# Seven-product stage of 17 granules, scores with a minimum per component, and other units in attention and memory of a hybrid trunk layer

## The chip, the cores and the metric

The kernel runs on one core of a Trainium2 chip. The metric is the device time of one execution in microseconds (us). TensorE (PE in the profile) multiplies matrices, VectorE (DVE) and ScalarE (ACT) work on what it leaves and prepare what it reads, GpSimd (POOL) and SyncE (SP) mostly issue DMAs.

## The reference, cut to what matters

One layer of a trunk over 640 tokens (512 latent tokens and 128 context tokens) of width 1024, in float32:

```python
x = x + 0.5 * m[2] * swiglu(hh, ffn1_w1, ffn1_w3, ffn1_w2)          # d_ff = 2816
mq, mk, mv, mo, mg, dq, dk, dv, gm, gd = split_cols(h @ w_in)
dq, dk = rope_2d(rmsnorm(dq)), rope_2d(rmsnorm(dk))                  # latent tokens only
pr = softmax(q_c . k_c * scale)  for components c = 0, 1             # 8 heads, 768 or 128 keys
att = (pr[0] - lam * pr[1]) @ v
h_f, h_b = mlstm_chunkwise(q, k, v, log_i, log_f, state)             # 4 heads of 256, both directions
hm = rmsnorm(h_f + h_b) * sigmoid(mo)
y = sigmoid(gm) * (hm @ w_br_m) + sigmoid(gd) * (att @ w_br_d)
x = x + m[5] * (y @ w_out)
x = x + 0.5 * m[8] * swiglu(hh, ffn2_w1, ffn2_w3, ffn2_w2)
```

The modulation vectors m come from silu(c) @ w_ada, a matrix of 1024 x 9216. The result must hold to float32 accuracy, so a product is made of three matmuls on split operands (high times high, high times low, low times high).

## The kernel before, in words

**Helpers.** Nearly every operation goes through a helper and carries its line: L54 is a DVE operation on two tensors, L57 one with a scalar as well, L61 one of a tensor and scalars, L51 an ACT activation, L75 a matmul, L78 a transpose by PE, L97 a load by SP. So groups are told apart by their tiles. DVE, ACT, PE and SP each work through their instructions in the order in which the program has them.

**Seven-product granules.** Large products are done as a two by two block product with seven products in place of eight (class `Winograd`). A granule is 256 output columns: 7 products of 12 matmuls 128x320 each, 84 in all. For that the weights are summed and split: ACT and DVE make `ww` (128x2048), `wB` (128x1024) and `wC` (128x512) out of the landed `raw`, and DVE forms the sums in `raw` (one add of 128x1024, two of 128x512). `u` and `t` are results of products on their way through ACT and DVE. In the same shape without that scheme, a granule is 4 units of 24 matmuls 128x320 (a feature unit) or 5 units of 24 matmuls 128x256 (a token unit).

**The stages in order of time** (read from the timelines): an opening (to about 90 us); FFN1's up products (to about 312); FFN1's down products (312 to 465), of which the middle part is four seven-product granules, `mid[0]` to `mid[3]`; the second norm and the first query and key projections (to about 505); the class `Gates`, a seven-product stage of 12 granules (505 to 655); attention (655 to 1079); the mLSTM ("memory", 1079 to 1210); the branch and output projections (to 1388); FFN2 (to the end).

**Gates** (L1783) computes gate columns for three of four groups (`gd`, `gm`), the four opening gates (`o`) and one query and one key granule of the mLSTM. Results go to DRAM (`g_out`). `between` (L1901) puts other work between its products: the rope (`qk_norm_rope`, L1470) of the first head pair's queries after granule 2 and of its keys after granule 3, and from granule 5 on four column tiles at the places `IN_GATES` (L1918). What the Tile scheduler makes of it is the order shown below.

**Column tiles** (`Columns`, L788): 56 tiles of 128 columns of the modulation product that are needed later. Each is a 512 KB load and two DVE operations over 128x1024 with a sum (L814, with a short read of the accumulator behind each). They are put wherever DVE has room: 11 in FFN1's up products, 9 and 4 in its down products (`TILES`, L1166, by granule and place), 4 in Gates, 8 in the memory stage (L2187), the rest in FFN2.

**Attention** walks 8 heads; a head has 5 blocks of 128 queries (`qi`). In a block: `scores` (L1597, 8 matmuls into a tile `sc` of 1536 columns over three PSUM banks, component 0 in its first half and component 1 in its second, then one minimum over both, L1617), `soft` (two exponentials on ACT, into tiles `p`, which read the minimum), `mix` on DVE, `turn` (6 transposes, `ps_wT`), `values` (12 matmuls, `ps_o`). The minimum, the exponentials and the mix stand between the matmuls of a block, so PE needs other work meanwhile: a queue of units (`Fill`), built from L1752 on, of which `UNITS` (L1954) says how many go into each block: mostly one in even heads, two in the first blocks of odd heads. The queue holds value projections (token units), keys and queries of pairs 1 to 3 (token units, each followed by its rope), and mLSTM queries and keys of heads 1 to 3 (feature units). At the end of a head the next head's `queries` and `keys` are turned; an odd head puts five single units there, an even one a group at each of three places. All of it shares a pool `ps2` of 5 PSUM banks.

**Memory** (class at L2037): for each of 4 heads a table `P` is loaded as a broadcast, masked, exponentiated and multiplied by key-query products (`prep`, `ps_st`), then 10 cells follow each other (`cell`). Three granules of units of 12 are left for it: the last key granule and the two of the gates (12 feature units).

## Time and profile before

| what | us |
|---|---|
| runs | 1814.38, 1814.83, 1815.23 (median 1814.83) |
| the profiled execution, and its span | 1815.7, and 1813.9 |
| PE busy, weight loads busy | 98%, 96% of the span |
| DVE, ACT busy | 74%, 50% |
| chain that ended last | PE 85%, DVE 7%, DMA 4%, ACT 2%, issue 1% |

A matmul's row shows its own duration, but matmuls overlap: 12 of 128x320 in a row start and end within about 1.8 us. So what an extra matmul costs is read from a long row of them, and what PE lost is read from the idle time in a stage. An idle time of PE is followed by the engine and tile that ended it.

### The profile page before, as it was taken

To read this page: it belongs to the slowest core of one execution; us is meant where nothing else is said; L and a number is where in the kernel's file an instruction comes from. 1 tells how busy PE (TensorE), PEld (TensorE's weight loads), DVE (VectorE), ACT (ScalarE), POOL (GpSimd) and SP (SyncE) were. 2 spreads that over 40 slices of the span, in tenths; PEclk is the share of its full clock that TensorE was granted. 3 is DMA by queue.
4 is the path that set the end of the run, shared out by engine and by line. 5 is a ranking of instruction groups with operands and counts; after the bars stand their busy time and mean duration, and the time that the engine had idled before them with its cause. 6 is when DMAs were issued, how large, how long until landed. Compare 5 with 4: busy or idle time off the path is not lost.

```text
span 1813.9 us, 30780 instructions
## 1 busy us (share of the span) xinstructions
PE 1785.6 (98%) x12550; PEld 1744.6 (96%) x12550; DVE 1349.6 (74%) x2178; ACT 910.8 (50%) x1588; POOL 39.2 (2%) x69
## 2 busy tenths in 40 slices
PE   8999999999999999999999999999999999999998
PEld 6999999999999999999999998899999999999998
DVE  6879987677888765858584557977767888897485
ACT  5654544333655445556564547674336545554432
POOL 0000000100000000000000000000000000000010
PEclk9999999999999999999999999999999999999999
DMA  8355566977245434221221124576642355557992
GB/s 326 111 198 171 186 236 221 350 227 266 83 139 181 160 131 143 78 69 63 69 69 55 68 81 163 182 257 218 221 171 80 134 173 185 203 180 274 353 311 80
DMA packets 132207, 311.36 MB, mean 172 GB/s; under 512 B 10017, under 2 KB 93217, under 8 KB 119009
## 3 DMA queue, kind: packets, MB, share of 16 engines
q1 hardware_dynamic: 121122, 265.22, 42.3%
q0 software_dynamic: 10256, 41.55, 7.1%
q8 instruction: 98, 1.61, 0.4%
q10 hardware_dynamic: 688, 2.63, 0.4%
q14 instruction: 43, 0.35, 0.1%
HBM read 240.49 MB, written 68.87 MB: 171 GB/s over the span
## 4 chain that ended last, share of the span: by engine, by line
PE 85%; DVE 7%; DMA 4%; ACT 2%; issue 1%; SPq 0%; DVEq 0%; ACTq 0%
PE ps_f L75 48%; PE ps_p L75 14%; PE ps_t L75 12%; PE sc L75 2%; PE ps_n L75 2%; PE ps_o L75 2%; DVE ww L54 2%; PE ps_u L75 1%; DMA raw_a<-in_w_ada_k 1%; PE ps_wT L78 1%; PE ps_qkT L78 1%; DMA raw<-in_w2b 1%; DVE junk L814 1%; DMA P<-nm_dram 1%; DVE mn L1617 1%
## 5 line engine op out<-in xcount | busy, mean ns | idle before, releaser
L75 PE MATMUL ps_f<-S,ww 128*128 128x320 f32 x2400 | 387.5, 310 | 5.2 <-DVE ww L54 1.9
L75 PEld LDWEIGHTS ps_f<-S,ww 128*128 128x128 f32 x2400 | 359.8, 188 | 9.6 <-DVE ww L54 6.5
L54 DVE TENSOR_TENSOR ww<-raw,ww 128x2048 fp32r<-128x2048 f32 (+1 forms) x73 | 163.9, 2246 | 74.3 <-ACT ww L51 74.2
L75 PE MATMUL ps_t<-wH,hH 128*128 128x256 f32 x640 | 185.7, 290 | 0.9 <-DVE x L57 0.9
L75 PE MATMUL ps_f<-hm,ww 128*128 128x320 f32 x1176 | 185.8, 309 | 0.1
L75 PE MATMUL ps_t<-wH,hL 128*128 128x256 f32 x640 | 181.6, 284 | 0.9 <-DVE hL L54 0.9
L75 PE MATMUL ps_t<-wL,hH 128*128 128x256 f32 x640 | 181.4, 283 | 0.0
L75 PEld LDWEIGHTS ps_f<-hm,ww 128*128 128x128 f32 x1176 | 175.7, 188 | 0.6 <-DVE ww L54 0.6
L51 ACT ACTIVATE ww<-raw 128x2048 fp32r<-128x2048 f32 (+1 forms) x73 | 136.9, 1875 | 60.3 <-DVE raw L54 33.0
L54 DVE TENSOR_TENSOR raw<-raw 128x1024 f32<-128x1024 f32 x186 | 161.0, 865 | 2.2
L75 PE MATMUL ps_f<-hm,wB 128*128 128x320 f32 x1008 | 161.5, 309 | 0.0
L75 PE MATMUL ps_p<-hH,wH 128*128 128x320 f32 x480 | 151.1, 315 | 0.7 <-ACT aT L51 0.7
L75 PEld LDWEIGHTS ps_f<-hm,wB 128*128 128x128 f32 x1008 | 151.3, 188 | 0.0
L75 PE MATMUL ps_p<-hH,wL 128*128 128x320 f32 x480 | 148.3, 309 | 0.0
L75 PE MATMUL ps_p<-hL,wH 128*128 128x320 f32 x480 | 148.3, 309 | 0.0
L51 ACT ACTIVATE u<-ps_f 128x320 f32<-128x320 f32 x129 | 55.8, 433 | 161.5 <-PE ps_f L75 159.7
L75 PEld LDWEIGHTS ps_t<-wH,hH 128*128 128x128 f32 x640 | 123.0, 192 | 1.5 <-ACT nsq L51 1.1
L75 PEld LDWEIGHTS ps_t<-wH,hL 128*128 128x128 f32 x640 | 122.9, 192 | 1.1 <-DVE hL L54 1.1
L75 PEld LDWEIGHTS ps_t<-wL,hH 128*128 128x128 f32 x640 | 123.1, 192 | 0.4
L1617 DVE TENSOR_REDUCE mn<-sc 128x2 f32<-128x1536 f32 (+1 forms) x40 | 59.5, 1489 | 56.0 <-PE sc L75 55.8
L54 DVE TENSOR_TENSOR wB<-raw,wB 128x1024 fp32r<-128x1024 f32 x64 | 78.1, 1221 | 26.7 <-ACT wB L51 26.7
L51 ACT ACTIVATE wH<-raw 128x2048 fp32r<-128x2048 f32 (+1 forms) x45 | 75.4, 1681 | 42.2 <-PE ps_p L75 35.5
(309 smaller groups left out, 3621.9 us busy)
## 6 DMA issues: line engine op xcount, KB each, us to landing
g_dram<-g SPq DMA_DIRECT2D x44, 640.0 KB, 7.6
raw_a<-in_w_ada_c POOLq DMA_DIRECT2D x35, 512.0 KB, 4.7
g_dram<-g SPq DMA_DIRECT2D x24, 480.0 KB, 8.1
raw<-in_w1b SPq DMA_DIRECT2D x11, 1024.0 KB, 4.9
raw<-in_w3b SPq DMA_DIRECT2D x11, 1024.0 KB, 6.3
raw<-in_w1a SPq DMA_DIRECT2D x10, 1024.0 KB, 4.9
raw<-in_w3a SPq DMA_DIRECT2D x10, 1024.0 KB, 6.2
hm<-g_dram SPq DMA_DIRECT2D x7, 1280.0 KB, 12.5
```

Of the source, the lines that this page charges most:

```text
L51: return placed(nc.scalar.activation(*args, **kw))
L54: return placed(eng.tensor_tensor(out=out, in0=in0, in1=in1, op=op))
L75: tc.keep_in_program_order(nc.tensor.matmul(*args, **kw))
L78: tc.keep_in_program_order(nc.tensor.transpose(*args, **kw))
L814: placed(vec.tensor_tensor_reduce(out=junk, in0=raw, in1=self.csil[:, v, :], op0=ALU.mult, op1=ALU.add, scale=1.0, scalar=0.0, accum_out=m ...
L1617: placed(vec.tensor_reduce(out=mn, in_=sv, axis=AX.X, op=ALU.min))
```

## The change

It has five parts.

- **Gates**: 17 granules in place of 12. The queries of heads 1 to 3 and the keys of heads 1 and 2 of the mLSTM move there from attention's queue, store to DRAM, and are loaded again: the keys of heads 0 to 2 late in attention (`load_keys` in head 6), the queries at the start of the memory stage (`load_queries`). Seven column tiles go between the products, not four. PSUM: four banks of `ps2`, and two halves of a tile `more` that later is the score tile of component 1 (class `Six`).
- **Scores**: each component has a PSUM tile of two banks and a minimum of its own (128x768), right behind its matmuls; `ps2` has 4 banks.
- **Attention's queue**: one mLSTM key granule (head 3) is left of the feature units; every block of every head has one unit; the ends of the heads are alike. Tiles of odd pairs' keys and queries have places of their own.
- **Memory**: values of head 3 (5 token units) come ahead of the two gate granules; two column tiles in place of eight; the query loads stand ahead of others on SP's queue.
- **FFN1's down products**: 12 column tiles in place of 9; `TILES` gets one more at each of (22, 1), (23, 0) and (23, 1).

```diff
-                    columns.place(9, places[0], load_columns_down, 4)
+                    columns.place(12, places[0], load_columns_down, 4)
...
-        TILES = {(21, 0): 2, (21, 1): 2, (22, 0): 2, (22, 1): 1, (23, 0): 1, (23, 1): 1, (28, 0): 2, (28, 1): 1, (29, 0): 1}
+        TILES = {(21, 0): 2, (21, 1): 2, (22, 0): 2, (22, 1): 2, (23, 0): 2, (23, 1): 2, (28, 0): 2, (28, 1): 1, (29, 0): 1}
...
-    psum = att.enter_context(tc.tile_pool(name="ps2", bufs=5, space=PSUM))
+    psum = att.enter_context(tc.tile_pool(name="ps2", bufs=4, space=PSUM))
...
+            n, self.n = self.n % 6, self.n + 1
+            return psum.tile(shape, dtype, tag=tag, name=name) if n < 4 else self.more[:, 512 * n - 2048 : 512 * n - 1536]
...
             for c in range(2):
+                s = ps_s.tile([128, 1024], F32, tag=f"s{c}", name="sc")
                 if qi < 4:
-                    for k0, k1 in (((0, 512), (512, 768)) if c == 0 else ((0, 256), (256, 768))):
+                    for k0, k1 in ((0, 512), (512, 768)):
...
-            placed(vec.tensor_reduce(out=mn, in_=sv, axis=AX.X, op=ALU.min))
+                placed(vec.tensor_reduce(out=mn[:, c : c + 1], in_=sv[c], axis=AX.X, op=ALU.min))
...
-            rest = [(a["w_mq"], mq_dram, 0, self.query), (a["w_mk"], mk_dram, 0, self.plain)]
+            qk = [(a[n], dst, h, f) for h in range(4) for n, dst, f in (("w_mq", mq_dram, self.query), ("w_mk", mk_dram, self.plain))]
...
-            for src, dst, g, f in gate[:4] + o[:1] + rest[:1] + o[1:2] + rest[1:] + o[2:3] + gate[4:5] + o[3:] + gate[5:]:
+            for src, dst, g, f in gate[:5] + qk[:3] + o[:1] + qk[3:5] + o[1:2] + qk[5:7] + o[2:] + gate[5:]:
...
-    IN_GATES = [(i, 1) for i in (5, 7, 9, 11)]
+    IN_GATES = [(i, 1) for i in (5, 6, 7, 9, 10, 12, 13)]
...
-    UNITS = {
-        0: (two, two, two, two, one, (1, 1, 1)), 1: (two, two, two, one, one, (0,)),
...
+    UNITS = {hd: (one,) * 5 + ((1, 1, hd < 4),) for hd in range(7)}
+    UNITS[7] = (one,) * 4 + ((0, 0), (0, 0))
...
+    in_pools["q"] = queries_of.enter_context(tc.tile_pool(name="mlq", bufs=1, side="right", reuse_waits="tile"))
+    load_queries(0)
...
-    columns.place(8, csil2, load_columns_raw, 1)
+    for h in range(1, 4):
+        load_queries(h)
+    columns.place(2, csil2, load_columns_raw, 1)
...
-            if n in ((3, 7), (2, 5, 8), (2, 5, 8), ())[h]:
+            if n in ((), (5,), (5,), ())[h]:
```

The order moves at three places of which the prediction speaks. The first is DVE in FFN1's down products, behind the split `ww` of `mid[0]`, up to the split of `mid[1]`. Before:

```order
L54 TENSOR_TENSOR ww<-raw,ww 128x2048
L54 TENSOR_TENSOR wB<-raw,wB 128x1024
L54 TENSOR_TENSOR wC<-raw,wC 128x512
L54 TENSOR_TENSOR raw<-raw 128x2x4x128
L54 TENSOR_TENSOR raw<-raw 128x4x128 x2
L57 SCALAR_TENSOR_TENSOR x<-ps_f,half_m,x 128x320
L54 TENSOR_TENSOR ww<-raw,ww 128x2048
```

And in the changed kernel, from the same split on:

```order
L54 TENSOR_TENSOR ww<-raw,ww 128x2048
L814 ISA ada,mod<-ada,csil 128x1024
L814 ISA mod 128x1
L54 TENSOR_TENSOR wB<-raw,wB 128x1024
L54 TENSOR_TENSOR wC<-raw,wC 128x512
L814 ISA ada,mod<-ada,csil 128x1024
L814 ISA mod 128x1
L54 TENSOR_TENSOR raw<-raw 128x2x4x128
L814 ISA ada,mod<-ada,csil 128x1024
```

Three more such operations follow, between the two small adds of `raw` and the residual's `x` and `t`, and then `ww` of `mid[1]`. So six column operations, as many as the three added tiles have, stand between the two splits, where there was none.

The second place is DVE in Gates, around the split `ww` of granule 5, with the rope of the first pair's keys (`k_tok`, `rope`, `ss`). Before:

```order
L54 TENSOR_TENSOR k_tok<-k_tok,ry 128x1280
L54 TENSOR_TENSOR g_out<-ps_f,u 128x320
L54 TENSOR_TENSOR k_tok<-k_tok,g_kn 128x256
L54 TENSOR_TENSOR ww<-raw,ww 128x2048
L61 TENSOR_SCALAR g_out<-ps_f 128x320
L54 TENSOR_TENSOR wC<-raw,wC 128x512
L54 TENSOR_TENSOR rope<-rope,ropeBk 128x1024
L54 TENSOR_TENSOR k_tok<-k_tok,ropeAk 128x1024
```

And now:

```order
L54 TENSOR_TENSOR k_tok<-k_tok,ry 128x1280
L54 TENSOR_TENSOR k_tok<-k_tok,g_kn 128x256
L54 TENSOR_TENSOR rope<-rope,ropeBk 128x1024
L54 TENSOR_TENSOR k_tok<-k_tok,ropeAk 128x1024
L54 TENSOR_TENSOR k_tok<-k_tok,rope 128x1024
L54 TENSOR_TENSOR ww<-raw,ww 128x2048
```

The three last steps of the rope stood behind the split and now stand ahead of it. One granule earlier the same holds for the queries' rope and the split of granule 4.

The third place is SP's queue at the start of the memory stage. Before:

```order
L97 DMA mask<-in_mask 128x256
L97 DMA P<-nm_dram 128x5x128 x2
L97 DMA va<-v_dram 128x5x256
L97 DMA C<-in_c_aug 128x516 x2
L97 DMA csil<-csil_dram 128x2048
L2049 DMA P<-nm_dram 128x5x128 x2
L2052 DMA va<-v_dram 128x5x256
```

And now:

```order
L1715 DMA mqT<-mq_dram 128x1280
L97 DMA mask<-in_mask 128x256
L97 DMA P<-nm_dram 128x5x128 x2
L97 DMA va<-v_dram 128x5x256
L97 DMA C<-in_c_aug 128x516 x2
L97 DMA csil<-csil_dram 128x2048
L1715 DMA mqT<-mq_dram 128x1280 x3
L1729 DMA v_dram<-stage 128x256 x2
L2026 DMA P<-nm_dram 128x5x128 x2
L2029 DMA va<-v_dram 128x5x256
```

Four query loads of 640 KB each, and two stores of values, now stand ahead of the second head's table `P`; on DVE the masking of that table moved from ahead of the first cell to behind the fourth.

## The prediction, on record before the changed kernel had run

> **What bounds the kernel now.** I read the page first. Its line of busy times and the line of the chain that ended last say the same thing:

> ```profile
> PE 1785.6 (98%) x12550; PEld 1744.6 (96%) x12550; DVE 1349.6 (74%) x2178; ACT 910.8 (50%) x1588; POOL 39.2 (2%) x69
> PE 85%; DVE 7%; DMA 4%; ACT 2%; issue 1%; SPq 0%; DVEq 0%; ACTq 0%
> ```

> PE is the bound. A change can gain in two ways: fewer matmuls, or fewer waits of PE. How much the waits are worth shows in the windows by stage (length, then busy time of PE, PE's weight loads, DVE, ACT, POOL). The four are FFN1's down products, Gates, attention from 750, and memory.

> ```profile
> 312.00:465.00 153.00, 151.65 (x1027) 150.46 (x1025) 107.08 (x167) 57.24 (x88) 11.87 (x19) 1.00 0.80 272
> 505.00:655.00 150.00, 148.36 (x1012) 148.09 (x1011) 115.73 (x158) 73.56 (x113) 2.11 (x4) 1.00 0.49 167
> 750.00:1079.00 329.00, 323.34 (x2547) 314.37 (x2545) 212.95 (x330) 179.22 (x379) 0.00 (x0) 0.99 0.19 64
> 1079.00:1210.00 131.00, 126.99 (x727) 113.93 (x727) 107.37 (x336) 86.91 (x222) 0.00 (x0) 1.00 0.58 183
> ```

> PE is idle for 1.35, 1.64, 5.66 and 4.01 us in them, 12.7 us together. That is all that removed waits can bring in the stages that the change touches, and it also says that PE has no slack there: a DVE that comes late shows on PE at once. The list of waits of PE names them (total, times, longest):

> ```profile
> PE ps_wT L78 <- DVE p L57: 3.0, 7, 0.8
> PE ps_f L75 <- DVE ww L54: 1.9, 3, 1.6
> PE sc L75 <- ACT p L51: 1.6, 3, 0.9
> PE ps_f L75 <- DMA S<-g_dram: 0.9, 1, 0.9
> PE ps_p L75 <- ACT aT L51: 0.7, 1, 0.7
> ```

> **The matmuls that go.** Five granules of mLSTM queries and keys leave attention, where each costs 4 units of 24 matmuls, and enter Gates, where each costs 7 products of 12. That is 96 against 84, so 60 matmuls of 128x320 fewer. Nothing else in the count of matmuls changes: the value units and the key granule that change places between attention and memory are whole in both kernels. The price of one comes from long unbroken rows of the chain (start, length, what):

> ```profile
> 275.42 100.31 PE ps_f L75 x682
> 754.84 3.51 PE ps_p L75 x24
> ```

> 100.31 / 682 is 0.147 us, and 3.51 / 24 is 0.146. So 60 x 0.147 = **-8.8 us**, on the engine that is the bound. This is the firm term.

> **Three more column tiles in FFN1's down products.** They bring six operations of L814 between the splits `ww` of `mid[0]` and `mid[1]`. DVE there before (start, length, what):

> ```profile
> 365.58 1.22 DVE L814 CUSTOM_DVE_ANT_0 ada<-ada,csil 128x1024 bf16<-128x1024 f32 x1
> 369.47 2.29 DVE L54 TENSOR_TENSOR ww<-raw,ww 128x2048 fp32r<-128x2048 f32 x1 [1.40 <-ACT ww L51]
> 372.14 1.23 DVE L54 TENSOR_TENSOR wB<-raw,wB 128x1024 fp32r<-128x1024 f32 x1 [0.37 <-ACT wB L51]
> 373.28 0.69 DVE L54 TENSOR_TENSOR wC<-raw,wC 128x512 fp32r<-128x512 f32 x1
> 373.88 2.67 DVE L54 TENSOR_TENSOR raw<-raw 128x1024 f32<-128x1024 f32 x3
> 377.52 0.55 DVE L57 SCALAR_TENSOR_TENSOR x<-ps_f,half_m,x 128x320 f32<-128x320 f32 x1 [0.96 <-PE ps_f L75]
> 379.00 2.29 DVE L54 TENSOR_TENSOR ww<-raw,ww 128x2048 fp32r<-128x2048 f32 x1 [0.94 <-ACT ww L51]
> ```

> and PE where it uses what that last split leaves:

> ```profile
> 380.83 2.24 PE L75 MATMUL ps_f<-hm,ww 128*128 128x320 f32 x12
> 383.98 1.99 PE L75 MATMUL ps_f<-S,ww 128*128 128x320 f32 x12 [0.90 <-DMA S<-g_dram]
> ```

> The split ends at 381.29, and PE's product from 380.83 on already waits a little for it (2.24 us; the 12 behind it have 1.99). Neighbouring instructions of DVE overlap by some 0.08, so I count the new order from 371.7: six column operations at 1.15, `wB` 1.14, `wC` 0.6, the adds 1.14 + 0.6 + 0.6, `x` 0.5, and `t` and two pieces of `x` (about 1.0), which now stand ahead of the split. That is 12.5, so the split starts at 384.2 and ends at 386.5, 5.2 later. Its ACT half is done by then, since `raw` is complete near 381. PE has nothing else to do in between, because its order is fixed. One thing is given back: the wait of 0.90 for a transfer at 383.98 lies behind and is covered. Sum **+4.3 us**. From below it could be 3 (if `t` and `x` went quicker), from above 6 (if one of the three tiles, which GpSimd loads, lands after its turn).

> **Gates.** The 17 granules themselves are in the first term. What is new is the order of the ropes. The rows of before that matter (the rope of the keys, the split of granule 5, the late split of granule 6, and the product that needs granule 5's split):

> ```profile
> 559.21 1.49 DVE L54 TENSOR_TENSOR k_tok<-k_tok,ry 128x1280 f32<-128x1280 f32 x1
> 561.35 2.29 DVE L54 TENSOR_TENSOR ww<-raw,ww 128x2048 fp32r<-128x2048 f32 x1
> 564.55 1.22 DVE L54 TENSOR_TENSOR rope<-rope,ropeBk 128x1024 f32<-128x1024 f32 x1
> 565.69 1.22 DVE L54 TENSOR_TENSOR k_tok<-k_tok,ropeAk 128x1024 f32<-128x1024 f32 x1
> 568.36 1.22 DVE L54 TENSOR_TENSOR k_tok<-k_tok,rope 128x1024 f32<-128x1024 f32 x1
> 577.42 2.29 DVE L54 TENSOR_TENSOR ww<-raw,ww 128x2048 fp32r<-128x2048 f32 x1 [1.39 <-ACT ww L51]
> 565.35 1.92 PE L75 MATMUL ps_f<-S,ww 128*128 128x320 f32 x12
> ```

> Granule 5's split ended at 563.64, 1.7 ahead of its use at 565.35. Now three steps of 1.22 stand ahead of it, 3.4 us net. One granule earlier the queries' steps do the same to granule 4. Walking both through with these lengths, granule 4's split comes about 0.9 late and granule 5's 2.2 later still: +3.1. Against that, the wait of 1.6 for the split at 577.42, which a column tile and two gate evacuations had delayed, goes, since the first column tile now comes after granule 6's split: I take -1.7, of the stage's 1.64 idle and the 1.9 of all such waits. Sum **+1.4 us**, from -1.7 (ropes covered) to +4.

> **Attention.** The minimum is split. Its rows, and the distance of two blocks with one unit (start of the scores):

> ```profile
> L1617 DVE TENSOR_REDUCE mn<-sc 128x2 f32<-128x1536 f32 x32 | 56.2, 1756 | 54.0 <-PE sc L75 54.0
> L1617 DVE TENSOR_REDUCE mn<-sc 128x2 f32<-128x256 f32 x8 | 3.4, 420 | 2.0 <-PE sc L75 1.9
> 806.50 1.40 PE sc L75 x8
> 812.76 1.40 PE sc L75 x8
> ```

> From 0.420 at 256 columns and 1.756 at 1536, a column costs 1.04 ns and an instruction 0.153 us, so half a tile costs 0.95 and two of them 1.91. The first half can start 0.7 earlier, behind half of the scores' 1.40. So the first exponential, which waited for the whole minimum, starts about 1.5 earlier. The longest wait for `p` is 0.8 and the waits for the score tile (`sc` for `p`) are at most 0.9, so both kinds, 4.6 us, can go. The price is 32 x 0.153 = 4.9 us of DVE, which has 329 - 213 = 116 us to spare in this stretch. [...]

> New waits come too. Heads 4 to 6 have no unit between the second half of the next keys and its scores, so PE waits for an evacuation by ACT; the nearest row is `ps_p` for `aT`, 0.7, three times: +2.1. And the rope of pair 1's queries is issued one block before they are packed. Its five steps take 1.49 + 0.42 (nearest row: the minimum of 256 columns) + 3 x 1.22 = 5.6 us of DVE beside the block's own 1.9 + 1.0 + splits, in a block of 812.76 - 806.50 = 6.3: 0 to 3 late, I take 1.5. Sum -4.6 + 2.1 + 1.5 = **-1.0**, from -4.6 (nothing new) to +4.9 (old waits stay and what DVE gained in work lands on PE).

> **Memory.** Four query loads of 640 KB now lie ahead of tables. DVE's maskings before, and the DMA view for 1079 to 1102:

> ```profile
> 1087.45 0.83 DVE L54 TENSOR_TENSOR P<-P,mask 128x640 f32<-128x640 f32 x1 [1.43 <-DMA P<-nm_dram]
> 1095.74 0.82 DVE L54 TENSOR_TENSOR P<-P,mask 128x640 f32<-128x640 f32 x1 [1.90 <-DMA P<-nm_dram]
> GB/s 0 0 334 236 277 217 86 140 142 151 150 221 311 361 395 398 453 429 446 435 340 358 346 290 281 267 342 346 306 272 253 226 328 385 374 241 144 75 41 14
> DMA packets 5089, 5.99 MB, mean 260 GB/s; under 512 B 224, under 2 KB 4320, under 8 KB 4960
> ```

> A load of 0.66 MB takes 1.4 us at the best slice (453 GB/s) and 2.5 at the mean (260). So head 0's table comes 1.4 to 2.5 later, and head 1's, behind all four, 5.8 to 10.1: from about 1096.5 to between 1102 and 1107. Its masking is now behind the fourth cell. The 40 cells of the stage fill 131 us, 3.3 each, so four of them behind a first table near 1090 end near 1103; I take 1104, an estimate. Against that stand six column tiles fewer (12 x 1.15 = 14 us of DVE), which should end small waits later in the stage, and PE's units, which fill the start. Sum **+0.3**, from -2 to +4.

> **The sum.** -8.8 + 4.3 + 1.4 - 1.0 + 0.3 = -3.8 us. The profiled execution took 1815.7 (span 1813.9, and 1.8 around it) and would take 1811.9; it lies 0.9 above the median of the runs, so the forecast for the median is 1814.8 - 3.8 = **1811.0**. About 0.2% (3.6 us) is what a measurement of this kernel can tell from no change, so 1811.2 to 1818.4 counts as the same: the forecast stands on the edge.

> **Rivals.**

> *The waits go and none comes* (chance 0.22). DVE is busy for 74% only; Gates' ropes hide, attention loses its 4.6 and gets 0.5 at most. -8.8 + 4.3 - 1.7 - 4.1 = -10.3: about 1804.5. For it speaks that the exponentials start 1.5 earlier; against it, that the splits in Gates had 1.7 to spare.

> *The gain is eaten* (0.17). Attention's new waits come at their upper end (+4) while the rest holds: -8.8 + 4.3 + 1.4 + 4 = +0.9, or with FFN1 at its lower end about 0: 1814 to 1816. For it speaks the packing of heads with one unit per block throughout.

> *The second head's table comes too late* (0.15). If the queue in front of it moves at the mean of 260 GB/s or below, it lands at 1107 or later. The masking stands on DVE ahead of every later cell of head 0, so all of them wait behind it from the fourth cell's end (1104) on. It decides from 1104; each us beyond is a us of PE once the units are used up. With 2.5 for head 0's table and 4 to 6 for head 1's, -3.8 + 8 = +4.2: 1819, slower.

> **Chances.** The forecast has 0.46, with a range of its own from 1807.5 to 1814.5; half of it lies below 1811.2. Faster by over 0.2%: 0.23 + 0.22 = 0.45. The same: 0.23 + 0.17 = 0.40. Slower: 0.15. The range reaches down to the first rival and up to the third's middle: 1804 to 1819.

> **What would show it.** In FFN1's down products the split of `mid[1]` ends near 386.5 and PE shows a wait of some 4 to 5 us for `ww` near 382. Gates shows two waits for `ww` near 554 and 567, and none in its later granules. In attention `ps_wT` for `p` and `sc` for `p` fall below 1 us in all. PE's matmul count is lower by 60. The forecast is wrong if FFN1's down stage is not longer by 3 us or more (then the kernel is nearer to 1806), or if a wait for `P` or `num` of over 3 us stands near 1100.

## The result, and the profile after

The changed kernel takes 1879.74 us (median of 4 runs, 1876.98 to 1882.14) against 1815.03 for the kernel before (4 runs, 1814.38 to 1817.99): 1.0353 times as long, with a 95% interval of 1.0332 to 1.0373. It is slower by 65 us. The forecast was 1811 and its upper end 1819.

PE has its 60 matmuls fewer, but it is busy for longer, and its share of the chain fell from 85% to 78%. The page of the changed kernel:

```profile
PE 1798.5 (96%) x12490; PEld 1752.8 (93%) x12490; DVE 1381.4 (73%) x2245; ACT 926.4 (49%) x1611; POOL 42.5 (2%) x75
PE 78%; DVE 9%; ACT 5%; DMA 4%; issue 3%; SPq 0%; DVEq 0%; ACTq 0%
```

Where the time went is seen by cutting both traces at the same places of the program: the first token product, the last gate column product, the last product of Gates, the end of attention, the end of memory. The windows of the kernel before (length; busy PE, weight loads, DVE, ACT, POOL; granted clock; DMA share and rate):

```profile
0.00:466.10 466.10, 456.98 (x3135) 444.45 (x3135) 364.73 (x539) 217.88 (x323) 18.05 (x34) 1.00 0.65 225
466.10:505.20 39.10, 37.74 (x292) 36.67 (x293) 36.19 (x58) 25.43 (x48) 0.00 (x0) 1.00 0.19 67
655.20:1079.00 423.80, 418.14 (x3340) 407.83 (x3338) 276.02 (x428) 232.32 (x485) 0.00 (x0) 1.00 0.23 76
```

and of the changed kernel:

```profile
0.00:473.20 473.20, 460.35 (x3134) 447.21 (x3135) 371.07 (x551) 217.58 (x322) 19.67 (x37) 0.99 0.65 225
473.20:518.40 45.20, 39.69 (x292) 38.65 (x293) 37.67 (x59) 28.04 (x50) 0.00 (x0) 0.92 0.27 90
518.40:763.10 244.70, 220.05 (x1432) 215.84 (x1431) 158.99 (x207) 99.56 (x151) 3.69 (x7) 0.97 0.41 137
763.10:1146.00 382.90, 354.06 (x2836) 342.87 (x2834) 267.38 (x457) 219.70 (x467) 0.00 (x0) 0.98 0.22 71
1146.00:1277.00 131.00, 127.12 (x754) 115.00 (x755) 97.26 (x314) 87.83 (x226) 0.00 (x0) 1.00 0.59 189
```

Gates was 150.0 long before. Five more granules of 84 matmuls at 0.147 us make 61.7, so it is 244.7 - 150.0 - 61.7 = 33.0 too long. Attention lost 5 x 96 x 0.147 = 70.6 us of matmuls (the five value units that leave it and the four key units that come to it have as many columns), so it should take 353.2 and takes 382.9, 29.7 too long. PE is idle there for 28.8 us, where it was idle for 5.7, so some 23 of the 29.7 are waits and the rest is PE's own pace. In one table, beyond the matmuls that were moved:

| stage | forecast, us | measured, us |
|---|---|---|
| up to the end of FFN1's down products | +4.3 | +7.1 |
| query and key token groups | 0 | +6.1 |
| Gates | +1.4 | +33.0 |
| attention | -1.0 | +29.7 |
| memory | +0.3 | 0.0 |

Behind memory the kernel is 0.5 us shorter (603.4 and 603.9). With the -8.8 of the matmuls this is the 66.5 us by which the span grew.

The list of PE's waits in the changed kernel names them (total, times, longest):

```profile
PE more L75 <- DVE g_out L54: 15.5, 10, 2.9
PE ps_o L75 <- ACT wT L51: 13.1, 5, 6.3
PE more L75 <- DVE g_out L57: 9.1, 6, 2.0
PE more L75 <- ACT k_tok L51: 5.0, 1, 5.0
PE ps_wT L78 <- DVE p L57: 4.1, 6, 1.4
PE ps_t L75 <- ACT v_tok L51: 4.1, 1, 4.1
PE ps_f L75 <- DVE ww L54: 3.1, 3, 2.8
PE sc L75 <- ACT kL L51: 2.9, 3, 2.1
```

Three of the first four are on `more`, the PSUM tile whose two halves serve Gates as two places. One of the 16 waits for `g_out`, PE's row and then DVE's row that ends it:

```profile
603.31 0.42 PE L75 MATMUL more<-hH,wB 128*128 128x320 f32 x1 [1.97 <-DVE g_out L57]
```

```profile
602.77 0.48 DVE L57 SCALAR_TENSOR_TENSOR g_out<-more,u 128x320 f32<-128x320 f32 x1
```

PE is ready at 601.3 and starts when DVE has read `more`. By the order in which the program hands out its places, the read is of the first half and the product goes into the second, in all 16. The halves lie 512 columns apart and belong to different granules; nothing in the data asks for this order.

### The profile page after: what moved, and what is told of

It reads as the page before. It is cut to its first block, busy times and chain, and to the rows that moved or that the text cites. A ratio compares the mean times of both kernels' runs of the same rounds, so it can differ in the third digit from the quotient of the medians.

```text
span 1880.4 us, 30924 instructions
## 1 busy us (share of the span) xinstructions
PE 1798.5 (96%) x12490; PEld 1752.8 (93%) x12490; DVE 1381.4 (73%) x2245; ACT 926.4 (49%) x1611; POOL 42.5 (2%) x75
## 4 chain that ended last, share of the span: by engine, by line
PE 78%; DVE 9%; ACT 5%; DMA 4%; issue 3%; SPq 0%; DVEq 0%; ACTq 0%
PE ps_f L75 43%; PE ps_p L75 11%; PE ps_t L75 10%; PE more L75 3%; PE sc L75 2%; PE ps_o L75 2%; DVE ww L54 2%; PE ps_n L75 2%; ACT ww L51 1%; DMA raw_a<-in_w_ada_k 1%; DVE junk L814 1%; PE ps_u L75 1%; PE ps_wT L78 1%; DMA raw<-in_w2b 1%; PE ps_qkT L78 1%
## 5 line engine op out<-in xcount | busy, mean ns | idle before, releaser
L75 PE MATMUL ps_f<-S,ww 128*128 128x320 f32 x2484 | 405.9, 312 | 2.3 <-ACT u L51 0.8
L75 PEld LDWEIGHTS ps_f<-S,ww 128*128 128x128 f32 x2484 | 378.3, 190 | 6.3 <-DVE ww L54 4.8
L54 DVE TENSOR_TENSOR ww<-raw,ww 128x2048 fp32r<-128x2048 f32 (+1 forms) x78 | 175.4, 2248 | 108.3 <-ACT ww L51 108.2
L75 PE MATMUL ps_f<-hm,ww 128*128 128x320 f32 x1176 | 187.4, 311 | 5.2 <-DVE ww L54 2.8
L51 ACT ACTIVATE ww<-raw 128x2048 fp32r<-128x2048 f32 (+1 forms) x78 | 146.4, 1876 | 92.1 <-PE ps_f L75 54.1
L75 PE MATMUL ps_t<-wH,hH 128*128 128x256 f32 x616 | 181.0, 294 | 8.6 <-ACT v_tok L51 4.1
L75 PEld LDWEIGHTS ps_f<-hm,ww 128*128 128x128 f32 x1176 | 176.9, 189 | 6.3 <-DVE ww L54 3.2
L75 PE MATMUL ps_t<-wL,hH 128*128 128x256 f32 x616 | 175.6, 285 | 0.0
L75 PE MATMUL ps_t<-wH,hL 128*128 128x256 f32 x616 | 175.5, 285 | 0.0
L54 DVE TENSOR_TENSOR raw<-raw 128x512 f32<-128x512 f32 (+1 forms) x201 | 173.5, 863 | 2.6
L75 PE MATMUL ps_f<-hm,wB 128*128 128x320 f32 x1008 | 161.5, 309 | 0.0
L75 PEld LDWEIGHTS ps_f<-hm,wB 128*128 128x128 f32 x1008 | 151.3, 188 | 0.0
L51 ACT ACTIVATE u<-ps_f 128x320 f32<-128x320 f32 x139 | 60.1, 433 | 166.2 <-PE ps_f L75 166.1
L75 PEld LDWEIGHTS ps_t<-wH,hH 128*128 128x128 f32 x616 | 119.4, 194 | 10.3 <-ACT v_tok L51 4.2
L75 PEld LDWEIGHTS ps_t<-wL,hH 128*128 128x128 f32 x616 | 119.7, 194 | 0.1
L75 PEld LDWEIGHTS ps_t<-wH,hL 128*128 128x128 f32 x616 | 119.2, 194 | 0.0
L54 DVE TENSOR_TENSOR wB<-raw,wB 128x1024 fp32r<-128x1024 f32 x69 | 84.1, 1219 | 38.1 <-ACT wB L51 38.1
L51 ACT ACTIVATE wB<-raw 128x1024 fp32r<-128x1024 f32 x69 | 72.6, 1052 | 59.2 <-DMA raw<-in_w2a 19.2
L75 PE MATMUL ps_p<-hH,wH 128*128 128x320 f32 x320 | 100.3, 313 | 0.0
L75 PE MATMUL ps_p<-hH,wL 128*128 128x320 f32 x320 | 98.9, 309 | 0.0
L75 PE MATMUL ps_p<-hL,wH 128*128 128x320 f32 x320 | 98.9, 309 | 0.0
L814 DVE CUSTOM_DVE_ANT_0 junk<-raw_a,csil 128x1024 bf16<-128x1024 f32 (+1 forms) x76 | 92.5, 1217 | 2.8 <-DMA raw_a<-in_w_ada_c 2.7
```

The source lines that it names most:

```text
L51: return placed(nc.scalar.activation(*args, **kw))
L54: return placed(eng.tensor_tensor(out=out, in0=in0, in1=in1, op=op))
L75: tc.keep_in_program_order(nc.tensor.matmul(*args, **kw))
L814: placed(vec.tensor_tensor_reduce(out=junk, in0=raw, in1=self.csil[:, v, :], op0=ALU.mult, op1=ALU.add, scale=1.0, scalar=0.0, accum_out=m ...
```

## The experiments

Theory H: a tile is the unit of the waits, so two halves of one tile that are used as two places wait for each other's readers. Its rival D: VectorE is too late in a stage of 17 granules. For attention, theory P (the PSUM layout with four banks and two minima) stood against theories U (the units and their order), A (ScalarE, which works in order, is held at a packing, for 3.39 us at the end of head 1) and C (there are too few units to cover a block's chain, that is, to give PE other work while the chain runs). Where one time is given for a run, it is a single execution, and the kernel before, run beside it, took 1816.5 (the first four experiments), 1817.0 (the next four) or 1813.5 (the two after them). So totals from different groups that differ by less than some 3.5 us are not told apart. The lengths of stages, cut as above, say more, though the first stage and memory vary by 2 to 3 us between runs that are alike there.

**Five places, of which one is a half of `more`.**

```diff
-            n, self.n = self.n % 6, self.n + 1
+            n, self.n = self.n % 5, self.n + 1
```

> The changed kernel with five accumulator places in Gates and the token groups: the four banks and only the first half of the tile `more`. Theory H (halves): a product into one half of `more` waits until VectorE has read the other half, since both are one tile; then all waits of PE for `g_out` on `more` (24.7 us in 16 waits) and the wait of 5.0 for `k_tok` go, and with them the slow clock behind the long ones: about 1843 to 1850. Theory D (VectorE is late in a stage of 17 granules with ropes and seven column tiles, and its evacuations hold the places): one place fewer makes it worse or no better: 1880 to 1895, the same waits on `ps_f`.

It took 1836.33 us, 43 less than the changed kernel and below the 1843 to 1850 of theory H, which had counted less for the clock and nothing for attention. The token groups, Gates and attention:

```profile
472.70:511.80 39.10, 37.61 (x292) 36.64 (x293) 36.21 (x57) 25.48 (x48) 0.00 (x0) 1.00 0.19 67
511.80:721.70 209.90, 209.90 (x1432) 209.76 (x1431) 159.79 (x211) 100.86 (x153) 3.69 (x7) 1.00 0.50 168
721.70:1100.20 378.50, 353.21 (x2836) 341.77 (x2834) 266.24 (x456) 219.16 (x466) 0.00 (x0) 0.98 0.22 70
```

Gates has no idle time of PE at all: 209.90 of 209.90 for the same 1432 matmuls that took 244.70. The token groups are back at 39.1. One place fewer made the stage 35 us shorter, which is H, and D has fallen: neither the ropes nor seven column tiles make a split late. The wait of 4.1 for `v_tok` at the start of attention went as well; which part of it was `more` and which a load on which ScalarE stood no run here tells apart.

**Six places in tiles of their own.**

```diff
-            self.n, self.more = 0, ps_s.tile([128, 1024], F32, tag="s1", name="more")
+            self.n, self.more = 0, [ps_x.tile([128, 512], F32, tag=f"x{i}", name="more") for i in range(2)]
...
-            return ... if n < 4 else self.more[:, 512 * n - 2048 : 512 * n - 1536]
+            return ... if n < 4 else self.more[n - 4]
```

> The changed kernel with the two halves made two tiles of one bank each (in a pool that is closed after Gates; the second score tile is opened then). The same banks, six places as in the changed kernel. Theory H: the waits for `g_out` go as in the run with five places, 1843 to 1850, and the sixth place adds nothing. Theory D: nothing changes, 1875 to 1882. A theory B (the two banks themselves collide with the reads): nothing changes either.

1838.61 us: Gates 211.7, token groups 39.0, and no wait for `g_out` in the list. So it is the tile, not the number of places and not the sixth place's bank. The sixth place adds nothing.

**The old PSUM layout and scores in the changed kernel** (five banks, one score tile of three banks with one minimum, no `more`).

```diff
-                s = ps_s.tile([128, 1024], F32, tag=f"s{c}", name="sc")
...
-                placed(vec.tensor_reduce(out=mn[:, c : c + 1], in_=sv[c], axis=AX.X, op=ALU.min))
+            s = ps_s.tile([128, 1536], F32, tag="sc", name="sc")
...
+            placed(vec.tensor_reduce(out=mn, in_=sv, axis=AX.X, op=ALU.min))
```

> The changed kernel with the PSUM layout and scores of the kernel before: five banks in the pool, one score tile of three banks, one minimum; no `more`. Gates should lose its waits for `g_out` under theory H. For attention, theory P (the layout: four banks, two minima) says that its 30 us of new loss go nearly all, about 1815 to 1822. Theory U (units and order: one unit in each block, the rope of a pair just ahead of its packing, ScalarE held by the packing) says that they stay: about 1840 to 1850, with ScalarE's `wT` again the largest wait of `ps_o`.

1842.31 us. Gates is 209.7, so H holds again. Attention is 386.9, longer by 8.4 than with the split scores (378.5). Theory P has fallen, and with the sign turned: the new layout does not cost attention its time, it saves 8 us of it. Which part of that is the two minima, and which the second score tile, no run here tells apart. What the list of waits has more here is `sc` for `p` (4.8 in 7 times, where the run with five places has none that the list shows) and `ps_aT` for `ao` (5.1).

**The new PSUM layout alone, in the kernel before** (`Six`, four banks, two score tiles and minima, 12 granules).

```diff
-    psum = att.enter_context(tc.tile_pool(name="ps2", bufs=5, space=PSUM))
+    psum = att.enter_context(tc.tile_pool(name="ps2", bufs=4, space=PSUM))
...
-    G = Gates(wide_p, ntmp, psum)
+    G = Gates(wide_p, ntmp, six)
```

> The kernel before with the new PSUM layout alone: four banks, the tile `more` in two halves for Gates' 12 granules and the token groups, two score tiles, two minima. Theory H: waits for `g_out` appear in the granules that use both halves, 1.5 us each, two for every second granule: 12 waits, some 18 to 20 us, and 5 to 6 in the token groups; 1835 to 1845. Theory D: with 12 granules and the old order VectorE is not late, so 1815 to 1820.

1849.94 us. The list of waits:

```profile
PE more L75 <- DVE g_out L54: 16.0, 8, 3.3
PE more L75 <- ACT k_tok L51: 5.0, 1, 5.0
PE more L75 <- DVE g_out L57: 3.3, 2, 2.2
```

Gates 176.0 in place of 150.0, the token groups 45.5 in place of 39.0. So the layout alone makes a loss of 33 us without any granule moved. The waits are what I expected, 19.3 us in Gates (10 of 1.9, where I had said 12 of 1.5) and 5.0 in the token groups; the total is above the 1845 that I had as the upper end, because PE is also slower behind them: in Gates the granted clock is 0.96 in the mean and PE is busy for 156.8 us with the matmuls that took 148.4. Attention is 423.9, the same as before: with the old units the new layout brings nothing.

**The three column tiles back from FFN1 to memory**, with five places (9 and 5 in place of 12 and 2).

```diff
-                    columns.place(12, places[0], load_columns_down, 4)
+                    columns.place(9, places[0], load_columns_down, 4)
...
-            if n in ((), (5,), (5,), ())[h]:
+            if n in ((), (2, 5, 8), (5, 8), ())[h]:
```

> Five places in Gates as before, and the three column tiles back from FFN1's down products to the memory stage (9 and 5 in place of 12 and 2). The stage up to the first token products took 472.8 with five places and 466.1 in the kernel before. Theory T (the tiles' six operations ahead of the second split): it goes back to about 466, and 1836.3 becomes 1829.5 to 1831. Rival M: the memory stage pays it back, +2 to +6 there, 1832 to 1836. Rival O: FFN1's loss has another cause and stays.

1835.47 us. FFN1's stages are back at 466.2 from 472.8, as theory T says. But the whole is only 0.9 shorter: memory takes 133.7 (130.7; the runs with two tiles there take 128.1 to 130.9), which is rival M, and attention 381.1 (378.5). In attention PE's idle time is 0.6 longer and its busy time for the same matmuls 2.0 longer (355.2 and 353.2), so most of this is a slower PE and not a new wait. In the run with both edits below the difference is 0.9.

**Packing one block later in odd heads**, with five places.

```diff
-            if qi == 3 and hd < 7:
+            if qi == 3 + hd % 2 and hd < 7:
```

> Five places in Gates, and in odd heads the packing of the next head's queries and keys one block later (after block 4, not 3). Theory A (ScalarE works in order: the packing waits for the rope, and the copies `wT` that `ps_o` needs stand behind it): the waits of `ps_o` for `wT`, 13.1 us, fall below 2 and with them the slow clock behind them: attention from 378.5 to about 364, the whole to about 1822. Rival R (the rope itself is late, and PE waits at the next transposes in place of `ps_o`): the wait moves to `ps_qkT`, attention stays above 373.

In the changed kernel this is the end of head 1, ACT and then PE:

```profile
869.17 1.06 ACT L51 ACTIVATE rope<-q_tok 128x1024 f32<-128x1024 f32 x1 [2.59 <-DVE q_tok L54]
870.14 0.38 ACT L51 ACTIVATE v_tok<-ps_t 128x256 f32<-128x256 f32 x1
873.91 0.74 ACT L51 ACTIVATE qpk<-q_tok 128x640 fp32r<-128x640 f32 x1 [3.39 <-DVE q_tok L54]
874.55 1.35 ACT L51 ACTIVATE kpk<-k_tok 128x640 fp32r<-128x640 f32 x2
875.81 0.85 ACT L51 ACTIVATE wT<-ps_wT 128x512 f32<-128x512 f32 x2
```

```profile
876.43 2.93 PE L75 MATMUL ps_o<-v_tok,wT 128*128 128x128 f32 x12 [6.33 <-ACT wT L51]
```

ACT stands at the packing `qpk` for 3.39 us, because DVE has not finished the rope of `q_tok`. Behind it in ACT's order are `kpk` and then `wT`, which has nothing to do with the rope and which PE needs. The later packing takes `wT` out of that place. It took 1826.89 us, 9.4 less, with attention at 371.6, where theory A had said 364 and rival R above 373. Theory A is right, but rival R for half of it: the waits of `ps_o` for `wT` fell from 13.1 to 0.9, and 5.9 came back at `ps_qkT`, as the list of waits says:

```profile
PE ps_qkT L78 <- DVE qpk L54: 5.9, 3, 4.5
PE ps_wT L78 <- DVE p L57: 4.9, 8, 1.4
PE sc L75 <- ACT kL L51: 3.6, 3, 2.1
```

**Both edits, and the three tiles in Gates in place of memory.**

> Both edits of the two runs beside it. If they are independent the gains add: 1836.3 - 6 - 14 = 1815 to 1818, the time of the kernel before. What is left of attention's loss should be the waits of 0.5 to 2.4 for `kL`, `p` and `ao`.

The second adds to that, in place of the edit of memory:

```diff
-    IN_GATES = [(i, 1) for i in (5, 6, 7, 9, 10, 12, 13)]
+    IN_GATES = [(i, 1) for i in (5, 6, 7, 8, 9, 10, 11, 12, 13, 14)]
```

> As both edits, but the three tiles go to Gates (10 there, 9 in FFN1's down products, 2 in memory). VectorE is busy for about 7 us of a granule's 12.3 there without a tile, and a tile adds 2.4: theory T says that Gates hides them, so 1814 to 1816, a little under the run with the tiles in memory. Rival: the splits come late in Gates as they do in FFN1 (a wait for `ww` in the granules with a tile), 1 us for each: 1817 to 1820.

1824.50 and 1821.69 us, both above what I expected (1815 to 1818, and 1814 to 1816). The gains of the two single runs had been 0.9 and 9.4 where I had put 6 and 14, so the first sum was too large, and the second stood on it. In the second the ten tiles leave Gates at 209.9, exactly as with seven. VectorE has that room in Gates and did not have it between the two splits of FFN1.

**Fifteen granules, and 8 units more in attention** (queries of heads 2 and 3 as feature units, `UNITS` with two units in the first blocks of heads 0, 1 and 3, and a third unit at the ends of heads 4 to 6).

```diff
-            ... gate[:5] + qk[:3] + o[:1] + qk[3:5] + o[1:2] + qk[5:7] + o[2:] + gate[5:]:
+            ... gate[:5] + qk[:3] + o[:1] + qk[3:4] + o[1:2] + qk[5:6] + o[2:] + gate[5:]:
...
+    for h in (2, 3):
+        feature(a["w_mq"][h], lambda h=h: query_store(h))
...
-    UNITS = {hd: (one,) * 5 + ((1, 1, hd < 4),) for hd in range(7)}
+    UNITS = {hd: (two if hd in (0, 1, 3) else one, two if hd < 2 else one) + (one,) * 3 + ((1, 1, 1),) for hd in range(7)}
```

> The run with tiles in Gates, but with 15 granules in Gates: the queries of heads 2 and 3 go back to attention's queue as 8 feature units (stored to DRAM, loaded later as before), which cover two blocks each of heads 0 and 1, one of head 3 and the ends of heads 4 to 6; column tiles 9 in FFN1, 9 in Gates, 3 in memory. It has 24 matmuls more (+3.5 us). Theory C (attention now waits since it has too few units to cover its chain): the waits at the start of head 1, for `qpk` and for `kL`, some 12 us with the slow clock, go: 1821.7 + 3.5 - 12 = 1811 to 1815. Rival V (VectorE's own work sets them: ropes, two minima, splits): they stay, 1823 to 1827.

1815.22 us, 6.5 less with 24 matmuls more; against the kernel before that ran beside each, +4.7 became +1.7, so of the 6.5 only 3.0 are safe as a total. The stages say it better. Attention with 17 granules, and then with 15:

```profile
715.90:1087.40 371.50, 351.40 (x2836) 340.06 (x2834) 265.50 (x456) 219.43 (x466) 0.00 (x0) 0.99 0.22 72
689.40:1080.80 391.40, 375.50 (x3029) 365.76 (x3027) 271.14 (x458) 225.51 (x476) 0.00 (x0) 1.00 0.23 77
```

Gates fell by 24.7 (185.2) and attention rose by 19.9 for 28.2 of matmuls: 8.3 us went, half of it idle time of PE (20.1 and 15.9) and half its pace. That is as theory C says, though by 8 and not by 12, and the time lies just above its range. The added units also put the rope further ahead of its packing, which is theory A; the next run holds the number of units fixed.

**Two units early, taken from two ends of heads**, with 17 granules.

```diff
-    UNITS = {hd: (one,) * 5 + ((1, 1, hd < 4),) for hd in range(7)}
+    UNITS = {hd: (two if hd == 0 else one,) * 2 + (one,) * 3 + ((1, 1, hd < 2),) for hd in range(7)}
```

> The run with tiles in Gates and 17 granules, with two units in head 0's first two blocks, taken from the ends of heads 2 and 3. No matmul more or less. If the distance from the rope of pair 1's queries to their packing is what counts (theory A), the wait of 4.5 for `qpk` at the end of head 1 goes and -6 us come with the clock behind it, less 1 to 3 for two more waits for `kL`: 1816 to 1819. Under theory C alone the cover is only moved: 1820 to 1823.

1822.45 us, no gain. The wait for `qpk` at the end of head 1 shrank from 4.5 to 1.2, as theory A has it, but a wait of 2.6 for a load (`ps_c` for `QQ`) came, those for `ao` grew from 1.5 to 3.6, and those for `kL` are 3.6 in five places in place of three. Attention is 374.2 (371.5). With the number of units fixed, the cover is only moved. That agrees with C.

**Fifteen granules with the packing where the changed kernel has it, and fourteen granules.** Against the run with 15 granules, the first and then what the second has besides (its four key units join attention's queue, and a column tile moves from Gates to memory):

```diff
-            if qi == 3 + hd % 2 and hd < 7:
+            if qi == 3 and hd < 7:
...
-            ... + qk[3:4] + o[1:2] + qk[5:6] + o[2:] + gate[5:]:
+            ... + qk[3:4] + o[1:] + gate[5:]:
...
-    UNITS = {hd: (two if hd in (0, 1, 3) else one, ...
+    UNITS = {hd: (two, ...
```

> The run with 15 granules, but with the packing in odd heads where the changed kernel has it (after block 3). With the added units the rope of a pair's queries ends two to three blocks ahead of its packing, so by theory A ScalarE is not held there any more and the three waits of `ps_qkT` for `qpk`, 1.2 us each, go as well: 4 us less than the run with 15 granules, 0.997 to 1.000 of the kernel before (1810 to 1814). Rival: ScalarE is held again as with 17 granules and the waits of `ps_o` for `wT` return: 1.002 to 1.006.

> As the run beside it, with 14 granules: the keys of head 2 go back to attention too, as 4 units that cover the first blocks of heads 2, 4, 5 and 6; column tiles 9, 8 and 4. It has 12 matmuls more (+1.8 us). Theory C: the waits at the starts of those heads, some 1.5 us each where the rope's steps stand ahead of the mix, shrink by 2 to 4: the same time within 2 us. Rival V: +1.8 and nothing gained.

Both were run 11 times, and the kernel before 21 times beside them. The first takes 1813.17 us against 1815.44, 0.9989 times the kernel before (interval 0.998 to 0.9997); the second 1814.38, 0.9997 (0.9988 to 1.0006). The first is the best version of this study, 2.3 us under the kernel before, a gain that its interval hardly tells from none. Attention is 387.9, 3.5 less than with the later packing, near the 4 that I expected. Its list of waits has no `ps_qkT` any more, and those of `ps_o` are small:

```profile
PE ps_wT L78 <- DVE p L57: 4.3, 5, 1.4
PE ps_t L75 <- DVE ao L61: 2.9, 2, 1.5
PE ps_o L75 <- ACT wT L51: 1.3, 3, 0.5
```

So the packing right behind a rope held ScalarE (3.39 us in the changed kernel), and the packing some blocks behind it left PE 1.3 us of waits for `wT` in all, in place of 13.1. Fourteen granules are no better: 1.2 us more, where theory C said the same time within 2 and rival V said 1.8 more, so the total does not tell them apart. The stage does: attention rose by 10.9 (398.8) for 14.1 of matmuls, so 3.2 us went from it, as C has it, and memory with its added tile is 2.2 longer. What is left is not explained: in the best version attention still takes 6.5 us more than the old stage does with the moved matmuls taken off (387.9 and 381.4).

## Why the prediction was wrong, point by point

**The matmuls.** Right: 60 fewer, and in the run with five places the whole of Gates shows what they cost, 209.90 us for 1432.

**The step that failed: Gates.** The prediction says "The 17 granules themselves are in the first term. What is new is the order of the ropes". New was also the tile in which two of six places lie. The change as I described it names "two halves of a tile `more`", and I gave it no price. It cost 33.0 us in Gates and 6.1 in the token groups. No row of the trace of before could show it, since there every place was a tile of its own; that called for bounds from both sides, and there were none. It is shown from both sides: the waits go when the two halves become two tiles or one of them is not used, and they come when the kernel before is given the halves. The ropes, which I did price at +3.1, cost nothing: with five places no split is late, and the old wait of 1.6 went as I said. The stage is then 1.8 below the old stage with the five granules added (211.7), which is about that wait. Of the two waits for `ww` that I named as a sign, near 554 and 567, none came.

**Attention, -1.0.** Wrong by 30 us. Of the old waits only one kind got its cure: `sc` for `p` (1.6) is gone, but `ps_wT` for `p`, which I had falling below 1, is 4.1 where it was 3.0. That the new layout is worth 8 us with the new units, and nothing with the old, is not what I had forecast for it either. The larger mistake is in the new waits. I took the rope of pair 1's queries as 1.5 late on PE's path. In fact its lateness stopped ScalarE at the packing, `wT` was queued behind, and PE waited for 6.3 and then ran at a granted clock of 0.50 (875.4 to 882.2). I priced the work on VectorE's queue, and did not name who is queued behind the instruction on ScalarE that waits for it. At heads 3 and 5 PE waited for `wT` too, 3.0 us each time: there the packing waited for nothing, but with about 1.9 us of its own (from 964.05 to `wT` at 965.95) it stood ahead of the copy all the same. And I set the work of DVE against a block's length in the mean; with 69 units where 90 were, there is no second unit to cover a block in which a rope falls. The run with 8 units more gave back 8.3 us. These steps name the larger part of the 30 us, and not all of it.

**FFN1's down products, +4.3.** The mechanism and the place were right:

```profile
383.67 0.76 PE L75 MATMUL ps_f<-hm,ww 128*128 128x320 f32 x2 [1.88 <-ACT ww L51]
387.21 3.04 PE L75 MATMUL ps_f<-hm,ww 128*128 128x320 f32 x10 [2.78 <-DVE ww L54]
```

```profile
370.26 2.29 DVE L54 TENSOR_TENSOR ww<-raw,ww 128x2048 fp32r<-128x2048 f32 x1 [1.40 <-ACT ww L51]
384.87 2.28 DVE L54 TENSOR_TENSOR ww<-raw,ww 128x2048 fp32r<-128x2048 f32 x1
```

The split ends at 387.15; I had put 386.5, and all of this trace runs 0.8 later from the opening on. PE's two waits make 4.7, inside the 4 to 5 that I said. Less the 0.9 that was given back, the waits are 3.8, near my 4.3. The term was mis-sized by the clock behind the waits, which is 0.52 in the mean from 384 to 391 and makes about 2.5 (7.1 less the other two), and 0.8 of the 7.1 comes from the opening.

**Memory, +0.3.** Right as a sum (131.0 and 131.0), and rival three has fallen: the second table's masking starts at 1170.2 without a wait. But the sum is a balance. A wait of PE of 1.5 for the first table `P` is new, and waits for `Cn` and `wv` (1.6 and 0.9) are gone, with six column tiles fewer. What the query loads alone cost no run here shows.

**The rivals.** The first had waits only go. The second named the packing of heads with one unit per block, which is one of the places where attention did lose, but it gave it +4 of the 30. The third, the only one that ended slower, had the wrong place, and +4 us where 65 came. None had a word on `more`.

## What to carry to other kernels

A buffer that is cut in two to serve as two places was one buffer here to whatever makes the waits (16 waits of 24.6 us together in Gates): give each place a tile of its own, or use one place fewer. When work is taken away from an engine that was covering others, count what it covered, block by block, and not only its time. And of an instruction that comes to wait, name first what stands behind it on its own engine: here ScalarE's copy for the next product, which had no part in the wait of 3.39 us, and for which PE waited 6.33.

## What the runs showed of the hardware that I had not expected

A wait of PE cost more than its length here. Behind the wait of 2.9 us that ends at 573.5 in the changed kernel the granted clock (the sixth number after the length) is 0.50 for the 3.2 us of the second row:

```profile
573.60:575.00 1.40, 1.40 (x10) 1.40 (x11) 1.40 (x3) 0.44 (x2) 0.00 (x0) 1.00 0.97 405
575.20:578.40 3.20, 3.20 (x13) 3.20 (x13) 2.95 (x6) 1.03 (x2) 0.00 (x0) 0.50 0.05 19
578.60:585.00 6.40, 5.57 (x38) 5.30 (x37) 6.08 (x5) 3.45 (x5) 1.05 (x2) 1.00 0.29 69
```

```profile
598.90:602.30 3.40, 2.44 (x17) 2.17 (x15) 3.40 (x6) 1.82 (x3) 0.29 (x1) 1.00 0.75 236
602.30:605.70 3.40, 2.39 (x16) 2.39 (x17) 3.33 (x5) 0.33 (x1) 0.24 (x1) 1.00 1.00 315
629.60:633.00 3.40, 1.48 (x10) 1.48 (x11) 3.37 (x6) 0.44 (x1) 0.53 (x1) 1.00 0.99 365
633.00:636.40 3.40, 3.40 (x15) 3.40 (x14) 1.02 (x2) 0.42 (x1) 0.00 (x0) 0.50 0.35 119
```

The first wait is cut in two by the grid, with 1.0 us of idle time on either side; the second lies in one cell, with 1.9 of 3.4 idle. In the traces of the two kernels, without their first 100 and last 20 us, there are nine cells at full clock in which PE was idle for 1.88 us or more, all in the changed kernel, and each is followed by one at 0.50. Of the cells at full clock with less idle time (up to 1.85) only one is (1.68, in the kernel before).

In Gates the slower pace shows in sum: PE is busy for 220.05 us in the changed kernel and for 209.90 with five places, with the same 1432 matmuls. The first 24.7 of the loss there are the waits, and the other 10.2 are a slower PE behind them: four stretches at half clock, at 1.3 to 1.7 us each (half of 3.41), make some 6 of it, and the rest is not traced.
